# The instructions of a diffusion layer's kernel, scheduled on a timeline model of the machine instead of the default model

## The chip, the cores and the metric

The kernel runs on one core of a Trainium2 chip. The metric is the device time in microseconds (us) of one launch; the median of several runs is given.

## What is computed

One layer of a diffusion backbone for 512 latent tokens and 256 context tokens of 1024 features, in float32: a half-step SwiGLU feed-forward, a token mixer, another half-step feed-forward on the latent tokens, and a final norm. All norms are modulated from a conditioning vector. Cut to what matters:

```python
def swiglu(h, w_in, w_out):
    g, u = jnp.split(h @ w_in, 2, axis=-1)
    return (jax.nn.silu(g) * u) @ w_out

def step(S, xs):                                   # scan over the chunks of 64 tokens, 8 heads, two directions
    u_n, w_n, qd_n, kd_n, aqk_n, bl_n = xs
    v_new = u_n - jnp.einsum('bhcd,bhde->bhce', w_n, S)
    o = jnp.einsum('bhcd,bhde->bhce', qd_n, S) + jnp.einsum('bhij,bhje->bhie', aqk_n, v_new)
    S = S * bl_n[..., None, None] + jnp.einsum('bhcd,bhce->bhde', kd_n, v_new)
    return S, o

def merge_branches(p, pool_diff, o, pool_w, pool_scale, gdn_norm_w, w_gdn_proj, w_pool_proj, w_mix_out):
...
    o = rmsnorm(o.astype(dt), gdn_norm_w) * jax.nn.silu(gate)
    y_gdn = o.reshape(B, L, GDN_WIDTH) @ w_gdn_proj
...
    g_pool, g_gdn = jnp.split(jax.nn.sigmoid(p[..., POOL_END:]), N_BRANCH, axis=-1)
    return (g_pool * y_pool + g_gdn * y_gdn) @ w_mix_out
```

## The kernel before

Activations lie with the feature on the partition and the token along the row. Every large product is made in float32r: an operand is split into a high part (a cast, `hi`) and a low part (the rest, `lo`), and three matmuls make one product. For weights this is done by `halves` (L114): a transfer brings 128 columns into a staging tile (`stg`, `qst`), ScalarE casts them to `whi` (L119), VectorE, or for some GpSimd, subtracts and gives `wlo` (L120). There are four buffers of each. For activations `ahi` (L188) and `alo` (L189) do the same.

**The feed-forward half-steps** (`ffn`, L419) multiply 2 x 2 blocks by seven products (Winograd): `quad_weights` (L292) lets GpSimd form sums of weight blocks (`qs`, L308 to L313), `quad` (L337) issues the products (matmuls L345) and VectorE combines the results (L354 to L370). The activation between the two projections is VectorE and ScalarE work (L257, L260, L474, L188, L189). The first half-step has the modulation's matmuls (`ada_steps`, L141; L150, L157) strewn in; the second, on the latent tokens alone, runs from about 1400 us to the end, with matmuls of 256 columns.

**The mixer** treats eight heads. For a head, `head` (L589) projects and convolves q, k and v, `front` (L757) makes norms and transposes, `invert` (L802) inverts the chunks' small systems, `scan` (L938) runs six steps, one behind another, both directions side by side. In a step of the scan PE multiplies the state S by k (L952) and q (L963), VectorE forms R (L956), PE multiplies with the inverse (L973), VectorE weights it (`vw`, L976), PE multiplies with k again (L985), and VectorE adds the result to S (L994). Behind the last step the output is normed, transposed (L1014), gated (`y`, L1016) and stored to DRAM (L1017). The scan of head k, the front of head k+2 and the inversion of head k+1 are written interleaved; behind them, in the same turn of the loop, come the jobs: the projections of head k+3 (`head`), the gate of head k+1 (`gate`, L1021), and, of 16 branch gates (`branch_gates`, L1026), as many as a list says:

```python
    ORDER = "sfifsisiissiis"
    SHARE = (3, 2, 0, 0, 0, 0, 0, 0, 6, 5)
```

Each job is `job` (L123): 24 matmuls of 512 columns (L132) for each part of the tokens, out of weights that wait for nothing of the scan. Its matmuls write the banks `b`, those of the scan the banks `g`, those of front and invert the banks `a`. Behind the mixer, the outputs come back from DRAM and the projections follow (L1060 to L1116).

**What sets the order.** The kernel is recorded under a context of the tile framework. A scheduler takes the recorded instructions and gives each engine its own sequence: of those that are ready by its model of the machine an engine takes the one that was written first. The engines then run their sequences in order, and wait on semaphores. The order on the chip is therefore what the scheduler's model of durations makes of the program.

Of the kernel before, what the change touches and what calls it, by code (L numbers as in the profile page):

```python
# [13 lines left out]
PSUM = bass.MemoryType.PSUM  # L14
# [27 lines left out]
def layer_kernel(ctx, tc, a, out):  # L42
# [64 lines left out]
    def weights(src, k0, nk, c0, engs=(act, dve)):  # L107
        """128 columns of a matrix, in two float32r parts."""
# [5 lines left out]
    def halves(w, first=act, second=dve):  # L114
        """Up to four feature tiles of 128 columns, in two float32r parts."""
# [7 lines left out]
    def job(w, act_hi, act_lo, ks, parts, new=None):  # L123
        """One tile of 128 output features: w (K on the partition) times the activations."""
# [40 lines left out]
    def mod_scale(n, k, mod, rn):  # L165
        """(1 + scale) * norm weight for feature tile k."""
        dve.tensor_scalar(out=eff[:, n, k, :], in0=mods[:, mod * 8 + k, :], scalar1=1.0,
                          scalar2=vec[:, 0, rn + k:rn + k + 1], op0=ALU.add, op1=ALU.mult)
# [5 lines left out]
    def rstd_of(ssq, n, dim):  # L174
        """ssq: [128, n] sums of squares with the token on the partition."""
# [23 lines left out]
    def rstd_rows(tmp, acc, parts, ssq=None, tag="b", dtag=("diag", 1)):  # L199
        """Root mean square, inverted, of every token, the same on all partitions."""  # L200
# [29 lines left out]
    # [C11 C12; C21 C22] = [A11 A12; A21 A22] [B11 B12; B21 B22], rows: two tiles of 128 output features,  # L230
    # columns: two halves of the tokens, inner: two halves of the 8 feature tiles
    def products(n2, more):
        """The places of the right-hand operands: B11, B21, B22, T4, T1, T2, T3, and B12."""
# [9 lines left out]
    def blocks_of(t, k, n2, dst):  # L243
        """The blocks of B themselves, of feature tile k."""
# [3 lines left out]
    def blocks(dst):  # L248
        """The operands of the products of the blocks themselves."""
        return lambda j, part, k: dst[(0, 7)[j] if k < 4 else (1, 2)[j]][part][:, k % 4]  # L250

    def combine(tmp, b11, b12, b21, b22, n2, put, bufs=1, eng=dve):
        """The other right-hand operands from the blocks; overwrites b12, and without bufs b11 and b22."""
# [19 lines left out]
    def side_by_side(ws, outs, rhs, ks):  # L273
        """Products of several weights, one feature tile k of all of them after another."""
# [7 lines left out]
    def plain(src, c0, rhs, n2, k0=0, nk=KT, tags=None):  # L282
        """As quad, by eight multiplications, from the blocks themselves."""
# [8 lines left out]
    def quad_weights(tmp, deep, src, c0, rows=None):  # L292
        """256 columns of src on their way to the seven left-hand operands, in the order of their use."""
# [3 lines left out]
        for i in range(2):  # L297
            # the inner halves: the first and the last four feature tiles, or the even and the odd ones
# [21 lines left out]
    class Quads:  # L320
        """The quads of a list of (src, c0, rows), one after another."""
# [15 lines left out]
    def quad(quads, gen, w1, w6, rhs, n2):  # L337
        """Two tiles of output features of all tokens: C11 (in PSUM), C12, C21, C22."""
# [155 lines left out]
    def last_pair(ahi, alo):  # L494
        """The last two feature tiles' share of the output, first for the latents, and the mixer's input from it."""
# [93 lines left out]
    def head(h):  # L589
        """Project, convolve k, q and v of one head."""  # L590
# [8 lines left out]
    # columns of the small arrays: (direction, chunk, head); chunks 0-3 latent, 4-5 context  # L599
# [88 lines left out]
    with tc.tile_pool(name="pb", bufs=1, reuse_waits="tile") as pb:  # L688
        # the pooled projection with the token on the partition
# [48 lines left out]
    # one on the diagonal of every 32 x 32 block; one for the first 16 partitions of every 32  # L738
# [18 lines left out]
    def front(h):  # L757
        """Norms of k and q of one head, k and v with the token on the partition."""
# [472 lines left out]
```

## Time and profile before

| | us |
|---|---|
| runs of the kernel before | 1804.62, 1804.71, 1808.05 |
| median | 1804.71 |
| span of the profiled execution, first to last instruction | 1807.2 |
| mean granted TensorE clock in it | 0.961 |

The profile is of one execution; its span is given, not a device time of its own, and lies between the runs. Engines are PE (matmuls of TensorE), PEld (its weight loads), DVE (VectorE), ACT (ScalarE), POOL (GpSimd) and SP (which issues transfers). L132 is line 132 of the kernel. A clock of 1.00 is the full TensorE clock. A time in brackets behind an instruction is how long its engine stood idle before it, with what released it. Tiles are named by the program: `b<-hhi,whi` writes a bank b from hhi and whi. Matmuls are pipelined: their pace is read from start to start, not from the duration of one.

### The profile page before, as it was taken

To read this page: it belongs to the slowest core of one execution; us is meant where nothing else is said; L and a number is where in the kernel's file an instruction comes from. 1 tells how busy PE (TensorE), PEld (TensorE's weight loads), DVE (VectorE), ACT (ScalarE), POOL (GpSimd) and SP (SyncE) were. 2 spreads that over 40 slices of the span, in tenths; PEclk is the share of its full clock that TensorE was granted. 3 is DMA by queue.
4 is the path that set the end of the run, shared out by engine and by line. 5 is a ranking of instruction groups with operands and counts; after the bars stand their busy time and mean duration, and the time that the engine had idled before them with its cause. 6 is when DMAs were issued, how large, how long until landed. Compare 5 with 4: busy or idle time off the path is not lost.

```text
span 1807.2 us, 34927 instructions
## 1 busy us (share of the span) xinstructions
PE 1649.1 (91%) x13432; PEld 1486.5 (82%) x13432; DVE 1365.7 (76%) x2647; ACT 943.9 (52%) x2088; POOL 632.3 (35%) x669
## 2 busy tenths in 40 slices
PE   6899999999999999899999999999987888888886
PEld 4798998989999778777877888777877888888886
DVE  5778888897878874457776778645549899899886
ACT  5533343434344465757777776564426444444454
POOL 2244434444534020332233321100005556555642
PEclk9999999999999999999999999999998999899988
DMA  9455455351212353522221212247431222222221
GB/s 272 117 147 160 133 144 156 110 161 62 76 59 71 117 169 120 130 64 60 53 59 47 67 40 66 59 132 224 129 105 48 77 88 83 82 82 85 79 82 59
DMA packets 250971, 184.06 MB, mean 102 GB/s; under 512 B 7008, under 2 KB 238133, under 8 KB 250677
## 3 DMA queue, kind: packets, MB, share of 16 engines
q1 hardware_dynamic: 250368, 181.65, 34.4%
q8 instruction: 106, 1.74, 0.4%
q14 instruction: 60, 0.49, 0.1%
q10 hardware_dynamic: 437, 0.18, 0.0%
HBM read 170.22 MB, written 11.58 MB: 101 GB/s over the span
## 4 chain that ended last, share of the span: by engine, by line
PE 55%; DVE 25%; issue 6%; ACT 5%; DMA 5%; POOL 2%; SPq 0%; POOLq 0%; ACTq 0%; DVEq 0%
PE b L132 12%; PE b L345 11%; PE g L345 7%; PE a L345 6%; DVE wlo L120 4%; DVE cv L583 2%; DVE q L474 2%; DVE alo L189 2%; PE b L279 2%; DVE t L257 2%; DVE xT L437 1%; PE a L708 1%; PE a L132 1%; PE b L150 1%; PE g L132 1%
## 5 line engine op out<-in xcount | busy, mean ns | idle before, releaser
L119 ACT CAST whi<-qst 128x512 fp32r<-128x512 f32 (+2 forms) x288 | 159.1, 554 | 164.7 <-PE b L345 66.7
L120 DVE TENSOR_TENSOR wlo<-qst,whi 128x512 fp32r<-128x512 f32 (+2 forms) x288 | 215.5, 757 | 16.7 <-ACT whi L119 16.4
L119 ACT CAST whi<-qs 128x512 fp32r<-128x512 f32 (+2 forms) x216 | 117.7, 554 | 171.4 <-POOL qs L309 82.1
L132 PE MATMUL b<-hhi,whi 128*128 128x512 f32 (+1 forms) x528 | 188.4, 386 | 0.0
L132 PE MATMUL b<-hlo,whi 128*128 128x512 f32 (+1 forms) x528 | 188.3, 385 | 0.0
L132 PE MATMUL b<-hhi,wlo 128*128 128x512 f32 (+1 forms) x528 | 187.7, 386 | 0.0
L308 POOL TENSOR_TENSOR qs<-qst 128x512 f32<-128x512 f32 (+2 forms) x72 | 92.7, 1287 | 253.1 <-DMA qst<-in_ffn_w_in_dram 70.2
L313 POOL TENSOR_TENSOR qs<-qst,qs 128x512 f32<-128x512 f32 (+2 forms) x72 | 87.4, 1214 | 198.1 <-DVE wlo L120 181.1
L119 ACT CAST whi<-stg 128x512 fp32r<-128x512 f32 x154 | 94.3, 620 | 112.7 <-PE b L132 70.4
L120 DVE TENSOR_TENSOR wlo<-qs,whi 128x512 fp32r<-128x512 f32 (+2 forms) x144 | 104.9, 728 | 49.7 <-ACT whi L119 49.4
L345 PE MATMUL b<-ehi,wlo 128*128 128x384 f32 (+1 forms) x240 | 84.3, 351 | 45.7 <-DVE wlo L120 45.7
L179 POOL TENSOR_TENSOR rs<-rs,mhalf 128x4 f32<-128x4 f32 (+2 forms) x13 | 14.0, 1077 | 294.6 <-DVE rs L177 279.0
L188 ACT CAST ahi<-q 128x384 fp32r<-128x384 f32 (+1 forms) x118 | 55.3, 473 | 118.1 <-DVE q L474 60.8
L583 DVE SCALAR_TENSOR_TENSOR cv<-raw,vec,cv 128x772 f32<-128x772 f32 (+1 forms) x96 | 100.4, 1046 | 11.6 <-ACT cv L581 8.3
L345 PE MATMUL g<-hhi,whi 128*128 128x384 f32 (+1 forms) x320 | 105.5, 330 | 2.5 <-ACT whi L119 2.5
L345 PE MATMUL g<-hhi,wlo 128*128 128x384 f32 (+1 forms) x320 | 103.6, 324 | 3.6 <-DVE wlo L120 3.6
L132 PEld LDWEIGHTS b<-hlo,whi 128*128 128x128 f32 x528 | 94.6, 191 | 14.9
L132 PEld LDWEIGHTS b<-hhi,whi 128*128 128x128 f32 x528 | 94.5, 191 | 14.9
L132 PEld LDWEIGHTS b<-hhi,wlo 128*128 128x128 f32 x528 | 94.0, 191 | 15.0
L345 PE MATMUL g<-hlo,whi 128*128 128x384 f32 (+1 forms) x320 | 103.6, 324 | 0.0
L120 POOL TENSOR_TENSOR wlo<-stg,whi 128x512 fp32r<-128x512 f32 x46 | 65.4, 1429 | 90.6 <-ACT whi L119 70.5
L312 POOL TENSOR_TENSOR qst<-qst 128x512 f32<-128x512 f32 (+2 forms) x72 | 95.6, 1327 | 0.6
(480 smaller groups left out, 5459.6 us busy)
## 6 DMA issues: line engine op xcount, KB each, us to landing
qst<-in_ffn_w_in_dram SPq DMA_DIRECT2D x80, 512.0 KB, 3.5
stg<-in_w_ada_dram SPq DMA_DIRECT2D x56, 512.0 KB, 4.6
stg<-in_w_mix_in_dram SPq DMA_DIRECT2D x49, 512.0 KB, 3.9
qst<-in_ffn_w_out_dram SPq DMA_DIRECT2D x40, 256.0 KB, 2.7
adx<-in_w_ada_dram SPq DMA_DIRECT2D x16, 512.0 KB, 7.1
qst<-in_ffn_w_out_dram SPq DMA_DIRECT2D x16, 512.0 KB, 3.8
crow<-cumd SPq DMA_DIRECT2D x16, 384.0 KB, 8.8
stg<-in_ffn_w_in_dram SPq DMA_DIRECT2D x8, 512.0 KB
```

What stands on the lines that cost most here:

```text
L119: (first.copy if first is act else first.tensor_copy)(out=hi[:, :n], in_=w)
L120: second.tensor_tensor(out=lo[:, :n], in0=w, in1=hi[:, :n], op=ALU.subtract)
L132: pe.matmul(res[p][:, :m], lhsT=ww(i), rhs=hh(k)[:, o:o + m], start=(i == 0 and j == 0), stop=(i == n - 1 and j == 2))
L188: act.copy(out=hi, in_=src)
L189: dve.tensor_tensor(out=lo, in0=src, in1=hi, op=ALU.subtract)
L257: eng.tensor_tensor(out=t, in0=x, in1=y, op=ALU.subtract)
L279: pe.matmul(x, lhsT=ww(k), rhs=rhs(j, part, k), start=n + e == 0, stop=n + e == len(ks) + 1)
L308: pool.tensor_tensor(out=s1, in0=a21, in1=a22, op=ALU.add)
L312: pool.tensor_tensor(out=a21, in0=a11, in1=a21, op=ALU.subtract)
L313: pool.tensor_tensor(out=s2, in0=a12, in1=s2, op=ALU.subtract)
L345: pe.matmul(o, lhsT=ww[:, k], rhs=rhs(j, part, k), start=first and k + i == 0, stop=k + i == nh + 1, skip_group_check=not first)
L583: dve.scalar_tensor_tensor(out=cv[:, :n], in0=raw[:, t:t + n], scalar=tap[t], in1=cv[:, :n], op0=ALU.mult, op1=ALU.add)
```

## The change

One argument of the context in the last function is added; it makes the scheduler use a timeline model of the machine for its durations. No instruction of the program is changed. The rest of the diff takes out comments and descriptions of functions, with line numbers kept.

```diff
-    with tile.TileContext(nc) as tc:
+    with tile.TileContext(nc, schedule_with_timeline_sim=True) as tc:
         layer_kernel(tc, aps, o)
```

The new order differs on every engine. The names in the rows below are the program's tiles: `S`, `R`, `vw`, `vn` belong to the scan of a head, `kf` and `qf` are its k and q, `b` is the bank of a job, `hhi` and `hlo` are the normed activations that all jobs read.

PE, in the scan of head 7, one step of it, before:

```order
L952 MATMUL g_14203<-S_14199,kf_12571 128x128 x2
L963 MATMUL g_14209<-S_14199,qf_12648 128x128 x2
L132 MATMUL b_14343<-hhi_72,whi_14339 128x512
L132 MATMUL b_14343<-hlo_73,whi_14339 128x512
L973 MATMUL g_14214<-R_14206,L_13424 128x128 x2
L132 MATMUL b_14343<-hhi_72,wlo_14340 128x512
L132 MATMUL b_14381<-hhi_72,whi_14373 128x512
L132 MATMUL b_14381<-hlo_73,whi_14373 128x512
L132 MATMUL b_14381<-hhi_72,wlo_14374 128x512
L132 MATMUL b_14381<-hhi_72,whi_14373 128x512
L132 MATMUL b_14381<-hlo_73,whi_14373 128x512
L985 MATMUL g_14222<-vw_14217,kt_12820 128x128 x2
```

The same step on PE in the change:

```order
L952 MATMUL g_14203<-S_14199,kf_12571 128x128 x2
L963 MATMUL g_14209<-S_14199,qf_12648 128x128 x2
L973 MATMUL g_14214<-R_14206,L_13424 128x128 x2
L997 MATMUL g_14209<-vn_14219,aqk_13425 128x128
L985 MATMUL g_14222<-vw_14217,kt_12820 128x128 x2
L997 MATMUL g_14209<-vn_14219,aqk_13425 128x128
L952 MATMUL g_14232<-S_14225,kf_12571 128x128 x2
```

The job matmuls between the scan's are gone from here. They stand earlier: this is PE in the change where the last of the mixer's jobs ends, in the scan of head 4, ahead of its output (L1014):

```order
L132 MATMUL b_14495<-hhi_72,whi_14491 128x512
L132 MATMUL b_14495<-hlo_73,whi_14491 128x512
L132 MATMUL b_14495<-hhi_72,wlo_14492 128x512
L997 MATMUL g_12495<-vn_12503,aqk_11275 128x128 x2
L924 MATMUL a_12541<-U_12301,x2_12539 64x64 x6
L917 MATMUL a_12549<-TN_12300,L_12075 64x64 x6
L926 MATMUL a_12558<-x2_12556,U_12301 64x64 x6
```

Behind this row no L132 stands until the mixer's 600 remaining matmuls are through: the rest of scan 4 with its output, the scans of heads 5, 6 and 7, the inversions of 6 and 7 and the end of 5, the front of 7. In the order before, the jobs' matmuls (14 jobs of them) stand interleaved with these to the end. On DVE and ACT the jobs' work (L120, L583, L119, L1032) leaves this stretch likewise.

DVE in the second half-step, a piece of the difference, at the weight part `wlo_17275`, for which PE waits at 1513.83 in the trace before:

```order
+L120 TENSOR_TENSOR wlo_17275<-qst_17182,whi_17274 128x512
+L474 TENSOR_TENSOR q_16480<-q_16480,q_17092 128x256
 L260 TENSOR_TENSOR q_16564<-q_16517,q_16564 128x256
-L474 TENSOR_TENSOR q_16480<-q_16480,q_17092 128x256
 L257 TENSOR_TENSOR t2_17222<-q_16517,t1_17219 128x256
 L189 TENSOR_TENSOR alo_17208<-t1_17219,ahi_17207 128x256
+L120 TENSOR_TENSOR wlo_17306<-qst_17184,whi_17305 128x512
+L354 TENSOR_TENSOR q_17253<-q_17253,b_17238 128x256
 L189 TENSOR_TENSOR alo_17208<-q_16480,ahi_17207 128x256
 L189 TENSOR_TENSOR alo_17208<-q_16564,ahi_17207 128x256
-L189 TENSOR_TENSOR alo_17208<-t2_17222,ahi_17207 128x256
-L120 TENSOR_TENSOR wlo_17275<-qst_17182,whi_17274 128x512
```

The subtraction that gives `wlo_17275` stood behind seven instructions of the activation and now stands ahead of them; nine such places repeat this. In the first half-step the modulation's matmuls (L150, L157) are moved some 22 matmuls forward on PE and spread over more places. ACT loads its function table 15 times instead of 13.

## Rows read from the trace of the kernel before

**Rows 1.** The page, busy us, share of the span, instructions.
```profile
PE 1649.1 (91%) x13432; PEld 1486.5 (82%) x13432; DVE 1365.7 (76%) x2647; ACT 943.9 (52%) x2088; POOL 632.3 (35%) x669
```

**Rows 2.** Busy us (xcount) by stretch; then granted clock, DMA share, GB/s.
```profile
100.00:400.00 300.00, 292.79 (x2259) 279.87 (x2258) 251.04 (x513) 117.00 (x250) 133.45 (x119) 1.00 0.49 143
700.00:1232.00 532.00, 500.45 (x5516) 416.29 (x5515) 348.90 (x822) 367.40 (x941) 127.83 (x234) 0.99 0.29 78
1080.70:1220.30 139.60, 135.89 (x1455) 111.60 (x1454) 86.88 (x226) 87.30 (x225) 15.59 (x29) 1.00 0.29 86
1400.00:1500.00 100.00, 87.89 (x677) 86.14 (x678) 92.20 (x146) 47.21 (x98) 58.52 (x45) 0.93 0.28 85
...
1400.00:1807.20 407.20, 340.98 (x2594) 333.84 (x2594) 356.64 (x555) 191.48 (x383) 215.54 (x153) 0.90 0.26 80
```

**Rows 3.** Timeline of DVE, outputs of heads 4 and 7: start, us, engine, line.
```profile
1079.94 0.75 DVE L1016 SCALAR_TENSOR_TENSOR y<-g,vec,sgate 128x512 f32<-128x512 f32 x1 [2.25 <-PE g L1014]
...
1219.52 0.75 DVE L1016 SCALAR_TENSOR_TENSOR y<-g,vec,sgate 128x512 f32<-128x512 f32 x1 [3.74 <-PE g L1014]
```

**Rows 4.** Stretch between these outputs, instructions of L132 and then of L120 alone.
```profile
1080.70:1220.30 139.60, 88.53 (x302) 52.84 (x303) 1.00 0.29 86
...
1080.70:1220.30 139.60, 16.61 (x25) 0.00 (x0) 1.00 0.29 86
```

**Rows 5.** Timeline of PE behind head 7 (in brackets: idle before, releaser).
```profile
1220.48 0.40 PE L132 MATMUL b<-hlo,whi 128*128 128x512 f32 x1
...
1228.45 0.40 PE L132 MATMUL b<-hhi,wlo 128*128 128x512 f32 x1
1232.21 0.51 PE L132 MATMUL b<-yphi,whi 128*128 128x512 f32 x1 [3.36 <-ACT yphi L188]
```

**Rows 6.** Timeline of DVE, then of PE, in scan 7.
```profile
1194.97 0.42 DVE L994 TENSOR_TENSOR S<-S,g 128x256 f32<-128x256 f32 x1 [0.89 <-PE g L985]
...
1197.68 0.42 DVE L976 TENSOR_TENSOR vw<-g,w 128x256 f32<-128x256 f32 x1 [0.80 <-PE g L973]
...
1199.72 0.42 DVE L994 TENSOR_TENSOR S<-S,g 128x256 f32<-128x256 f32 x1 [0.70 <-PE g L985]
...
1195.54 0.68 PE L952 MATMUL g<-S,kf 128*128 128x128 f32 x4
...
1198.97 0.71 PE L985 MATMUL g<-vw,kt 128*128 128x128 f32 x4
```

**Rows 7.** A stretch of 20 us in which PE waits, columns as rows 2.
```profile
1340.00:1360.00 20.00, 12.77 (x49) 9.25 (x48) 9.90 (x19) 6.01 (x12) 2.65 (x3) 0.75 0.32 97
```

**Rows 8.** Waits of PE, 1400 to 1807 (total us, times, longest); its timeline.
```profile
PE b L345 <- DVE wlo L120: 40.1, 10, 4.8
...
1423.29 0.58 PE L345 MATMUL b<-ehi,wlo 128*128 128x256 f32 x1 [4.76 <-DVE wlo L120]
...
1719.58 0.58 PE L345 MATMUL b<-ehi,wlo 128*128 128x256 f32 x1 [4.26 <-DVE wlo L120]
```

**Rows 9.** Timeline of DVE, then of POOL, before 1513.83.
```profile
1502.09 0.42 DVE L474 TENSOR_TENSOR q<-q 128x256 f32<-128x256 f32 x1
...
1507.85 1.18 DVE L260 TENSOR_TENSOR q<-q 128x256 f32<-128x256 f32 x1
...
1510.35 1.48 DVE L257 TENSOR_TENSOR t<-q,t 128x256 f32<-128x256 f32 x1
...
1512.76 0.41 DVE L189 TENSOR_TENSOR alo<-t,ahi 128x256 fp32r<-128x256 f32 x1
1513.10 0.68 DVE L120 TENSOR_TENSOR wlo<-qst,whi 128x512 fp32r<-128x512 f32 x1
...
1504.46 1.41 POOL L313 TENSOR_TENSOR qs<-qst,qs 128x512 f32<-128x512 f32 x1 [4.22 <-DVE wlo L120]
...
1510.11 1.45 POOL L312 TENSOR_TENSOR qst<-qst 128x512 f32<-128x512 f32 x1
```

**Rows 10.** Waits of PE, 0 to 420 us.
```profile
PE b L150 <- DMA stg<-in_w_ada_dram: 1.5, 4, 0.6
```

## The prediction

> **What bounds the kernel now.** I start with the busy times of the whole span: TensorE's matmuls (PE) fill 91% of it, VectorE (DVE) 76%, ScalarE (ACT) 52% [rows 1]. That average covers two regimes, so the second view is the busy times by stretch. From 100 to 400 us (first feed-forward half-step) PE is busy 292.8 of 300 us. In the mixer, 700 to 1232, it is 500.5 of 532: 31.6 us idle. From 1400 to the end (second feed-forward half-step) it is only 341.0 of 407.2, and there DVE is the busier one with 356.6 [rows 2]. The third view, single instructions and their idle time, says why the mixer is dense although its scan is a chain that waits at every step: between the scan's small matmuls PE runs the large ones of `job` (L132), which need nothing of the scan. The output of head 4 (L1016) ends at 1080.7, that of head 7 at 1220.3 [rows 3]; between them there are 302 of these matmuls [rows 4], and 35 more behind head 7, the last at 1228.45 [rows 5].
>
> I take 1804.7, the median shown, as the base; the profiled span is 1807.2, 0.1% above. About 0.2% (3.6 us) is what a measurement of this kernel can tell from no change.
>
> **The change, part by part.** No matmul or vector instruction is added or removed, ACT gets two table loads more (no row prices them here; they are bounded by 0 and a few us, which the other ends swallow), so the whole effect is one of order.
>
> *1. The mixer's jobs run out early.* In the new order of PE the last L132 matmul of the mixer stands ahead of head 4's output transposes, and behind them come 600 matmuls of chains alone: scans 5, 6 and 7, inverts 6 and 7. So 302 + 36 matmuls move ahead of head 4's output. Their pace is (1228.45 − 1220.48)/34 = 0.234 us from start to start [rows 5], so they take 338 × 0.234 = 79 us. They can sink only into what PE has idle before: of the 31.6 us, 3.7 lie inside the tail itself (139.6 − 135.9) and 3.4 at the wait of 1232.21 [rows 2, 5]; that leaves 24.5, and I take half of it, since the rest stands where jobs were to be had already. Head 4's output thus ends 79 − 12 = **+67 us** later than 1080.7 (ends: +55 and +79).
>
> *2. The tail without cover.* The stretch from head 4's output to head 7's took 139.6 us [rows 2]; what would it take with the jobs gone? Below it can't fall under its own work: PE 135.9 − 302 × 0.234 = 65 us, DVE 86.9 less 16.6 for the jobs' weight splits (L120) = 70 [rows 2, 4]. Above stands its old length. Between these I read the step of scan 7 [rows 6]. From S at 1194.97 to S at 1199.72 is 4.75 us. In it the jobs delay the chain: vw ends at 1198.10, but its matmul L985 starts at 1198.97, 0.87 later, while L952, which waits for nothing else, starts at 1195.54, 0.15 after S ended at 1195.39. So 0.72 of a step of 4.75 is queueing behind jobs, and a step without them is 4.0, 0.84 of the old. I apply this to the whole tail: 0.84 × 139.6 = 117. [...] About half of a step is matmuls, so I add 5%: 123 us, and the tail gives back **−17 us** (ends: −64 at 75 us, +7 at 147).
>
> *3. Behind head 7* PE has 35 job matmuls left, then waits 3.36 for the reloaded y; the first projection starts at 1232.21 [rows 5]. Without jobs and with their weights long cast the next stage can begin sooner, unless the transfer of y sets it: **−4 us** (ends −8 and 0).
>
> *4. Second feed-forward half-step.* Nine times PE idles some 4.5 us at 128x256 matmuls `b<-ehi,wlo` because the weight part wlo (L120) isn't there; the first (4.76) and the last (4.26) of them are in [rows 8], and the view of waits counts 40.1 us in ten there, nearly all of it these nine. The wait's cause is in the row of DVE: wlo's subtraction itself takes 0.68 us but stands behind seven activation instructions, the first at 1507.85, the last at 1512.76 [rows 9]. The new DVE order puts the wlo ahead of them at all nine places. So the waits as they stand are ordered away, up to −40. But then DVE is late next: it would have to do its 356.6 us in 367, 97% busy, and no 100 us stretch of it that I read shows over 92.2% [rows 2]. At 92.2% its work takes 387, which is **−20 us**; I take that (ends: 0 and −40). DVE isn't free to be denser: an L257 instruction takes 1.48 us there while POOL runs, an L474 of the same shape 0.42 when POOL rests [rows 9].
> [...]
>
> *5. First feed-forward half-step.* The modulation matmuls (L150, L157), a compact block before, start about 22 matmuls sooner and are spread. PE waits for their transfer hardly at all now: 1.5 us in four waits, 0.6 the longest [rows 10]. If each of some 23 blocks in 100 to 400 waited 0.6, that would be +14; PE's idle time there is 7.2, which bounds a gain at −7. I take **+3**.
>
> **The sum**: 67 − 17 − 4 − 20 + 3 = +29, so 1804.7 + 29 = **1834 us**. It is slower because the jobs were not a load beside the scans but their filling: moved ahead, they lengthen a stretch that was full, and the chains that they leave are not much shorter for it.
>
> **The rivals.**
> *A, faster: the tail shrinks to its work.* If the chains of heads 5, 6 and 7 run side by side once no job stands between, the tail is set by DVE's 70 us, say 75 with joints, 48 less than forecast: 1834 − 48 = 1786. It decides at 123 − 29 = 94 us: a tail shorter than that makes the change faster. For it: DVE and ACT are lighter there by the jobs' casts. Against it: in the new order scan 6 begins behind scan 5's output, and a scan's six steps follow one another through S. Chance 0.09.
> *B, much slower: nothing is given back.* The tail keeps its 139.6 us with the 5% of a lower clock (147, 24 more), and the second half-step stays as long as it was, DVE being the bound there (20 more): 1834 + 24 + 20 = 1878. For it: the 0.75 of the clock at an idle PE [rows 7], and DVE at 88 to 92% [rows 2]. Against it: the jobs' queueing in front of L985 is real and ends. Chance 0.19.
> *C, no change: PE's work decides.* PE is at 91% [rows 1] and its work stays the same; idle time is merely dealt out otherwise, some in the mixer, less in the half-step behind, and the gain of step 4 meets the loss of steps 1 to 3 at 1805. It asks for a mixer loss of about 26, which is 20 less than mine (a tail of 103 us). Chance 0.06.
> [...]
>
> **How the numbers follow.** The forecast has 0.66, with a range of its own of 1812 to 1858 (the tail between 101 and 147, or step 4 between 0 and −40, one at a time); A 0.09, B 0.19, C 0.06. The range that leaves out the far half of A and of B, about 2 in 10 with the forecast's own misses, is 1800 to 1876. Faster by over 0.2%: A, 0.09. Within: C, 0.06. Slower: 0.85.
>
> **What would show it.** Right: no L132 between head 4's output (L1016) and head 7's; that output of head 4 at about 1148, head 7's at about 1270, the tail near 123 us with PE idle for half of it and a granted clock below 1; the nine waits on wlo shortened, DVE above 90% behind 1450. Wrong: a tail under 94 us (A), long waits `b<-ehi,wlo` still there under other names (B), head 4's output less than 40 us later, which would mean that PE had room before it, or new waits of L150 on its transfers in the first 400 us.

## The result and the profile after

The changed kernel takes 1945.3 us (median of 4 runs, 1940.6 to 1947.2); the kernel before took 1806.4 beside it. The ratio is 1.0756, 95% interval 1.073 to 1.078: slower, as forecast, but by 139 us where 29 were forecast, and outside the range of 1800 to 1876.

The page of the kernel after, its line of busy times (to be held against [rows 1]):

```profile
PE 1725.1 (89%) x13432; PEld 1532.4 (79%) x13432; DVE 1408.1 (72%) x2647; ACT 945.8 (49%) x2090; POOL 636.0 (33%) x669
```

The same 13432 matmul records are busy for 1725 us in place of 1649: no work was added, yet TensorE is busy 76 us longer. That goes with a lower granted clock (0.88 for 0.98 in the mixer), as the stretches show. Busy times by stretch of the kernel after, columns as in [rows 2]: the first feed-forward half-step, the mixer, 32 us inside the mixer, the stretch from head 4's output to head 7's, and two stretches of the second half-step:

```profile
100.00:400.00 300.00, 298.11 (x2196) 268.18 (x2195) 257.82 (x498) 114.61 (x243) 131.03 (x115) 1.00 0.47 139
600.00:1383.00 783.00, 673.83 (x6183) 565.19 (x6183) 433.63 (x983) 431.26 (x1041) 140.21 (x266) 0.88 0.25 72
953.00:985.00 32.00, 22.88 (x315) 19.58 (x315) 21.11 (x59) 16.44 (x43) 4.13 (x7) 0.73 0.15 42
1250.20:1382.60 132.40, 91.42 (x1104) 76.87 (x1102) 68.14 (x196) 63.11 (x170) 14.17 (x26) 0.71 0.09 31
1600.00:1700.00 100.00, 86.31 (x688) 83.85 (x688) 97.06 (x152) 47.83 (x102) 61.84 (x46) 0.98 0.29 93
1540.00:1944.90 404.90, 340.62 (x2651) 329.23 (x2649) 372.72 (x568) 193.38 (x394) 223.86 (x158) 0.95 0.26 81
```

and the mixer's stretch in the kernel before, with the same view:

```profile
585.00:1220.30 635.30, 598.75 (x6151) 500.69 (x6150) 427.90 (x979) 421.46 (x1034) 145.19 (x266) 0.98 0.30 85
```

The mixer is 783 us long in place of 635. PE's idle time in it rose from 36.5 to 109 us, and its busy time for the same matmuls from 599 to 674, at a granted clock of 0.88 in place of 0.98. So half of the 148 us shows as waits and half as longer busy time; what the lower clock costs the chain is read at experiment 8. DVE, in the second half-step, is now busy for 97% of a stretch of 100 us.

By stage, from the ends of the heads' outputs (L1016) and of the last L345 and L708 matmuls, before and after:

| | before | after | difference of the stage |
|---|---|---|---|
| first half-step ends (last L345) | 585.4 | 600.0 | +14.6 |
| last L708, before the heads | 697.7 | 739.1 | +26.8 |
| output of head 0 | 845.0 | 933.7 | +47.3 |
| output of head 3 | 1022.3 | 1156.8 | +45.8 |
| output of head 4 | 1080.7 | 1250.2 | +35.0 |
| output of head 7 | 1220.3 | 1382.6 | −7.2 |
| second half-step begins (first L345) | 1386.4 | 1540.6 | −8.1 |
| end | 1807.2 | 1944.9 | −16.5 |

Each column is one profile. The first half-step ended at 589.9 and 589.4 us in experiments 4 and 13, which leave it in the order of before, and at 597.6, 595.9 and 595.9 in 6, 8 and 15, which leave it in the order of the change: its difference is some 6 to 15 us. The stage between head 7's output and the second half-step took 162.4 us in 4 and 13, in the same order as the 166.1 above.

The rows for the outputs of heads 0, 4 and 7 in the kernel after, timeline of DVE (compare [rows 3]):

```profile
932.91 0.75 DVE L1016 SCALAR_TENSOR_TENSOR y<-g,vec,sgate 128x512 f32<-128x512 f32 x1 [0.40 <-PE g L1014]
...
1249.50 0.75 DVE L1016 SCALAR_TENSOR_TENSOR y<-g,vec,sgate 128x512 f32<-128x512 f32 x1
...
1381.84 0.75 DVE L1016 SCALAR_TENSOR_TENSOR y<-g,vec,sgate 128x512 f32<-128x512 f32 x1 [3.99 <-PE g L1014]
```

The loss arises before head 4's output. Two views of the kernel after say how: the matmuls of jobs alone (L132), over the period from head 0's output to head 1's and over 32 us in it (compare [rows 4]; columns PE, PEld, clock, DMA share, GB/s):

```profile
932.90:1006.60 73.70, 30.56 (x146) 23.62 (x147) 0.88 0.15 44
953.00:985.00 32.00, 0.64 (x3) 0.19 (x1) 0.73 0.15 42
```

The period has 146 job matmuls, nearly as many as before (158 in the period of 60.7 us), but none in its middle (the three counted there end by 953.7, the next starts at 988.0): for 32 us PE runs the chain alone, and it is busy there for 22.9 us only, at a granted clock of 0.73. The order of TensorE says the same. Between the outputs of heads 0 and 3 the jobs' matmuls stand in 79 runs of 5.6 on average before, with never more than 102 chain matmuls between two runs; in the change they stand in 28 runs of 15, with three stretches of some 170 chain matmuls, one to a head, without a job (a chain matmul leaves two records in the trace: the two L952 of a step are x4 in [rows 6]).

### The profile page after: what moved, and what is told of

The parts are those of the page before. It is cut to its first block, busy times and chain, and to the rows that moved or that the text cites. A ratio compares the mean times of both kernels' runs of the same rounds, so it can differ in the third digit from the quotient of the medians.

```text
span 1944.9 us, 34914 instructions
## 1 busy us (share of the span) xinstructions
PE 1725.1 (89%) x13432; PEld 1532.4 (79%) x13432; DVE 1408.1 (72%) x2647; ACT 945.8 (49%) x2090; POOL 636.0 (33%) x669
## 3 DMA queue, kind: packets, MB, share of 16 engines
q8 instruction: 106, 1.74, 0.4%
## 4 chain that ended last, share of the span: by engine, by line
PE 39%; DVE 14%; ACT 6%; issue 4%; DMA 2%; POOL 0%; SPq 0%; ACTq 0%; POOLq 0%; DVEq 0%
PE b L132 16%; PE b L345 4%; DVE wlo L120 3%; PE g L345 2%; PE a L345 2%; DVE q L474 1%; PE g L132 1%; PE g L973 1%; PE g L952 1%; PE a L708 1%; DVE alo L189 1%; PE a L132 1%; ACT din L848 1%; PE g L997 1%; PE g L985 1%
## 5 line engine op out<-in xcount | busy, mean ns | idle before, releaser
L120 DVE TENSOR_TENSOR wlo<-qst,whi 128x512 fp32r<-128x512 f32 (+2 forms) x288 | 250.0, 872 | 16.7 <-ACT whi L119 16.4
L119 ACT CAST whi<-qst 128x512 fp32r<-128x512 f32 (+2 forms) x288 | 157.9, 554 | 174.1 <-PE b L345 91.0
L132 PE MATMUL b<-hhi,whi 128*128 128x512 f32 (+1 forms) x528 | 189.6, 380 | 8.9 <-ACT cv L576 5.5
L132 PE MATMUL b<-hlo,whi 128*128 128x512 f32 (+1 forms) x528 | 187.3, 377 | 0.0
L119 ACT CAST whi<-qs 128x512 fp32r<-128x512 f32 (+2 forms) x216 | 118.0, 552 | 140.7 <-POOL qs L309 45.0
L132 PE MATMUL b<-hhi,wlo 128*128 128x512 f32 (+1 forms) x528 | 186.2, 376 | 0.0
L308 POOL TENSOR_TENSOR qs<-qst 128x512 f32<-128x512 f32 (+2 forms) x72 | 94.1, 1307 | 225.3 <-DMA qst<-in_ffn_w_in_dram 67.4
L119 ACT CAST whi<-stg 128x512 fp32r<-128x512 f32 x154 | 93.6, 619 | 93.0 <-PE b L132 58.7
L583 DVE SCALAR_TENSOR_TENSOR cv<-raw,vec,cv 128x772 f32<-128x772 f32 (+1 forms) x96 | 94.9, 988 | 43.2 <-ACT cv L581 19.4
L132 PEld LDWEIGHTS b<-hhi,whi 128*128 128x128 f32 x528 | 96.6, 191 | 29.2 <-ACT cv L576 7.3
L120 DVE TENSOR_TENSOR wlo<-stg,whi 128x512 fp32r<-128x512 f32 x108 | 75.1, 702 | 59.6 <-ACT whi L119 54.5
L120 DVE TENSOR_TENSOR wlo<-qs,whi 128x512 fp32r<-128x512 f32 (+2 forms) x144 | 105.3, 731 | 8.3 <-ACT whi L119 8.2
L132 PEld LDWEIGHTS b<-hhi,wlo 128*128 128x128 f32 x528 | 95.3, 191 | 17.0
L132 PEld LDWEIGHTS b<-hlo,whi 128*128 128x128 f32 x528 | 95.8, 191 | 16.4
L345 PE MATMUL g<-hhi,wlo 128*128 128x384 f32 (+1 forms) x320 | 101.2, 316 | 4.8 <-DVE wlo L120 4.8
L345 PE MATMUL g<-hhi,whi 128*128 128x384 f32 (+1 forms) x320 | 102.5, 320 | 1.9 <-ACT q L352 1.9
L345 PE MATMUL g<-hlo,whi 128*128 128x384 f32 (+1 forms) x320 | 100.5, 314 | 0.0
L312 POOL TENSOR_TENSOR qst<-qst 128x512 f32<-128x512 f32 (+2 forms) x72 | 100.2, 1392 | 0.6
L120 POOL TENSOR_TENSOR wlo<-qs,whi 128x512 fp32r<-128x512 f32 (+2 forms) x72 | 91.0, 1264 | 27.7 <-ACT whi L119 27.5
```

The lines of the kernel that those rows point to most:

```text
L119: (first.copy if first is act else first.tensor_copy)(out=hi[:, :n], in_=w)
L120: second.tensor_tensor(out=lo[:, :n], in0=w, in1=hi[:, :n], op=ALU.subtract)
L132: pe.matmul(res[p][:, :m], lhsT=ww(i), rhs=hh(k)[:, o:o + m], start=(i == 0 and j == 0), stop=(i == n - 1 and j == 2))
L308: pool.tensor_tensor(out=s1, in0=a21, in1=a22, op=ALU.add)
L312: pool.tensor_tensor(out=a21, in0=a11, in1=a21, op=ALU.subtract)
L345: pe.matmul(o, lhsT=ww[:, k], rhs=rhs(j, part, k), start=first and k + i == 0, stop=k + i == nh + 1, skip_group_check=not first)
```

## The experiments

Most kernels below take one of the two programs and fix the order of an engine in a stage to a table. The function is the same in all; the table is a list of the program's instruction numbers.

```python
    def follow(eng, names):
        """Issue the instructions of one engine in the order of this table (order alone, no wait)."""
        by = {i.name: i for i in nc.cur_bb.bb.instructions}
        seq = [by["I-%d" % n] for n in names if "I-%d" % n in by]
        for first, then in zip(seq, seq[1:]):
            tc.add_manual_dep(then, first.name,
                              mybir.DependencyInfo(mybir.DependencyClass.NoSync, mybir.DependencyReason.DATA),
                              reason="order")
```

What isn't in a table the scheduler of that kernel orders anew around it; this matters below.

**1 and 2. TensorE's order in the mixer, old in the new kernel and new in the old one.**

```diff
+    follow(None, table(ORDER_0))   # 1: TensorE, mixer, order of the kernel before; 2: of the changed kernel
```

> The changed kernel with TensorE's order in the mixer (3899 matmuls) fixed to that of the kernel before; all other engines and stages are scheduled by the timeline model. Theory A (TensorE's new order clusters the jobs' matmuls, so the chains run bare and at a lower clock): the mixer's 148 us come back, about 1797 us, between 1785 and 1815. Theory B (the new order of VectorE, ScalarE and the transfers slows the mixer): it stays above 1900.

> The kernel before with TensorE's order in the mixer fixed to that of the changed kernel, nothing else. Theory A: the mixer loses what it lost in the change, 148 us, about 1950 us, between 1925 and 1965. Theory B: below 1840.

Measured: 1875.3 and 1984.4 (ratios to before 1.036 and 1.097, intervals 1.032 to 1.041 and 1.092 to 1.102). Both miss the ranges of their theories; Theory A holds for the sign and not for the size. Putting TensorE's old order into the changed kernel gives back 70 us and not 148; putting the new one into the old kernel costs 177, more than the whole change. In experiment 1 the periods up to head 5's output are 62 to 71 us, near the old 56 to 61, but the stretch behind head 4 takes 154 us, against 139.6 before and 132.4 in the change: TensorE, in its old order, waits for results of VectorE and ScalarE, whose orders are new. The waits of PE in that kernel, 600 to 1304 us, its two largest:

```profile
PE g L952 <- DVE S L994: 14.6, 10, 2.7
PE g L997 <- ACT vn L980: 9.3, 8, 2.6
```

against 5.1 and 1.4 in the kernel before. An order of one engine carries a part of the effect. That a misfit with the others' orders comes on top is how these waits are read; no run isolates it.

**5 and 12. More engines' orders put back.** Both are kernel 1 with further tables.

```diff
     follow(None, table(ORDER_0))   # TensorE
+    follow(None, table(ORDER_1))   # VectorE (12); in 5 two tables more, for ScalarE and GpSimd
```

> The changed kernel with the order of TensorE, VectorE, ScalarE and GpSimd in the mixer fixed to that of the kernel before; transfers and the other stages stay as the timeline model orders them. With TensorE's order alone fixed, 69 us of the mixer's 148 stayed. Theory A (the orders of VectorE and ScalarE make the rest): about 1806 us, between 1795 and 1820. Theory B (the rest is in the transfers' order): above 1850.

> The changed kernel with the orders of TensorE and VectorE in the mixer fixed to those of the kernel before, ScalarE and GpSimd free. With TensorE alone 1875, with all four 1822. Theory A (VectorE is the partner whose order has to fit): below 1840. Theory B (it is ScalarE): above 1858.

Measured: 1822.6 with four engines (ratio 1.008, 1.005 to 1.011), 1853.9 with TensorE and VectorE (1.025, 1.021 to 1.028). With all four (just above the range of Theory A) the heads are what they were: periods of 58 to 61 us up to head 4, 139.4 from head 4 to head 7. The mixer as a whole takes 651 us, 16 more than before: 11 lie ahead of the heads and 5 up to head 0's output. So the engines' orders make some 132 of the mixer's 148 us, and at most the 16 are left for the transfers' order, which stayed new. Put back behind TensorE's, VectorE's order is worth 21 of the 53 us between kernels 1 and 5, ScalarE's and GpSimd's the other 31; neither theory of 12 is right alone.

**14. Jobs in lumps, in the old kernel.** TensorE's own old order, with the matmuls of each job put together.

```diff
+    follow(None, table(ORDER_0))   # TensorE, mixer: old order, each job's 24 or 48 matmuls at the place of the middle one
```

> The kernel before, with TensorE's order in the mixer fixed to its own, except that the matmuls of each of the mixer's jobs (24 or 48) stand together at the place of the middle one: 45 runs in place of 246. Nothing else is moved. Theory A (the fine interleaving is what hides the chains; a lump of 24 holds a chain step up by 5.6 us): 40 to 110 us slower, 1850 to 1920. Theory B (only the rough distribution of the jobs over the heads counts): within 15 us of 1807.

Measured: 1994.5 us, ratio 1.103 (1.101 to 1.105), 185 us slower: beyond the range of Theory A. A head's period is 77 to 83 us in place of 58 to 61, and the stretch from head 4 to head 7 is 188 in place of 140. Busy times of this kernel from head 1's output to head 2's, and from head 4's to head 7's:

```profile
976.60:1059.20 82.60, 67.94 (x686) 57.74 (x686) 43.78 (x102) 45.26 (x117) 17.69 (x29) 0.83 0.15 39
1216.50:1405.00 188.50, 158.48 (x1445) 130.44 (x1444) 86.04 (x222) 85.58 (x217) 15.41 (x29) 0.87 0.20 62
```

The number of matmuls is that of [rows 2] in the second stretch (x1445 against x1455), the jobs lie in the same places on the scale of a head, and PE is idle for 30 us and busy for 22 more. A run of 24 matmuls is 24 x 0.234 = 5.6 us [rows 5], longer than a whole step of the scan (4.75 us [rows 6]). What a chain step behind a run meets can be read in the kernel after, ahead of head 1's output: ScalarE has written vn (L981) at 989.50, but the L997 that takes it starts at 993.13, 3.63 us later, and in between PE is busy without a break with the matmuls ahead of it in the sequence, 17 L132 (988.01 to 992.25) and those of an inversion (from 992.18).

But more was moved than TensorE's matmuls. The other engines are ordered anew around the table: of the mixer's instructions only 76% on VectorE and 80% on ScalarE still stand in the succession of the kernel before (the longest that the two traces share; 95% and 98% in experiment 5). So the 185 us are the lumps together with the new orders around them, and no run parts the two.

**15. Jobs spread, in the new kernel.** The converse, for three heads.

```diff
+    follow(None, table(ORDER_0))   # TensorE, mixer: new order, 77 job matmuls of each period put in ones to threes into the bare chain
```

> The changed kernel with TensorE's order in the mixer fixed, but between the outputs of heads 0 and 3 the 77 job matmuls of each period that stood in runs ahead of a bare chain of 170 matmuls are spread over that chain, in ones to threes. Theory A (bunched jobs and bare chains run one after the other): each of the three periods falls from 74 us by 6 to 14, in all 1903 to 1927 us. Theory B (the periods are set by the orders of VectorE and ScalarE): periods of 70 us and more, above 1935.

Measured: 1931.7 us (ratio 1.068, 1.066 to 1.070), 14 us below the change. The three periods fell from 73.7, 76.3 and 73.1 to 67.4, 72.9 and 67.4, so by 6.3, 3.4 and 5.7: the right direction, the low edge or less of Theory A, and none near the 58 of before; the total lies between the two theories. The granted clock of the three periods went from 0.88, 0.80 and 0.88 to 1.00, 0.93 and 0.97. VectorE and ScalarE stay close to the change's orders here (93% and 95% by the count used for 14). So bunching on TensorE is a cause in the new order, for 15 of the 46 us lost between these outputs, and not the only one there.

**6 and 9. The last branch gates held for heads 5 to 7.** In 6 the first matmul of each of 11 gates is held behind a step of a scan, and the scheduler places the rest; in 9 the same 264 matmuls lie in 42 pieces where PE stood idle.

```diff
+    for step, gate_ in zip([...], [...]):          # 6: 11 scan matmuls, 11 first matmuls of a gate
+        tc.add_manual_dep(by["I-%d" % gate_], "I-%d" % step,
+                          mybir.DependencyInfo(mybir.DependencyClass.NoSync, mybir.DependencyReason.DATA), reason="order")
+    follow(None, table(ORDER_0))                   # 9 in its place: TensorE, mixer, the gates' matmuls in the gaps
```

> The changed kernel with the last 11 branch gates held on TensorE behind steps of scans 5, 6 and 7 (one edge of order each), so that they lie again between the chains. Theory A (the chains leave room that these 264 matmuls, 62 us, fill): head 4's output comes some 62 us sooner, the stretch from it to head 7's stays within 132 to 150 us, in all 1885 to 1905 us. Theory B (TensorE is no less busy for it, the chains slow down by what they cover): above 1930.

> The changed kernel with TensorE's order in the mixer fixed, and its 264 matmuls of the last 11 branch gates (62 us) taken out of it and put, in 42 pieces of 1 to 24, into the places where TensorE stood idle in the trace of heads 5 to 7 (39 us in all), in proportion to the idle time. Theory A (held in lumps of 24 they cost their full length, in pieces as long as the gaps they are nearly free): head 4's output some 46 us sooner, the stretch behind it 132 to 158 us, in all 1900 to 1925 us. Theory B (these matmuls cost their length wherever they stand, because other engines or the weights hold them): above 1935.

Measured: 1942.6 and 1930.0 us. In 6, head 4's output came 50 us sooner (the period 48.0 in place of 93.5), and the stretch behind it took it all back: 181.8 in place of 132.4. The gates, there in 25 runs of up to 24, cost as much as they had cost ahead of head 4. In the 42 pieces (9) the stretch behind head 4 grew by 14.8 us for the 62 of work, but head 4's output came only 29 us sooner; the total lies between the two theories, 15 us below the change. The finer cut cost less; it also lies in other places, so how much of this is the size of the pieces is not shown, nor that small pieces are nearly free.

**7. L997 behind L985 again.** In the new order one L997 stands ahead of L985 in the scan's steps.

```diff
+    follow(None, table(ORDER_0))   # TensorE, mixer: new order, in steps 2 to 4 of each scan L985 x2 ahead of L997 x2
```

> The changed kernel with TensorE's order in the mixer kept, but L997 (output matmuls of a scan step, waiting for ScalarE's vn) behind L985 (the state's) as it stood before; three steps of each of eight scans. Theory A (L997 in front holds the state's chain up by 0.5 to 0.8 us a step): 24 steps, 10 to 19 us faster, 1926 to 1936. Theory B (vn and vw come at the same time, or other waits end last): within 4 us of 1945.

Measured: 1953.6 us (1947.4 to 1956.0), no faster, rather 8 us slower: Theory A falls, and the 4 us of Theory B are passed too. The trace of this kernel says why, in scan 7: DVE's vw, ACT's two halves of vn, and PE's L985, now first in its queue:

```profile
1367.22 0.42 DVE L976 TENSOR_TENSOR vw<-g,w 128x256 f32<-128x256 f32 x1 [1.31 <-PE g L973]
...
1367.95 0.26 ACT L981 COPY vn<-g 128x128 f32<-128x128 f32 x1
...
1368.26 1.22 PE L985 MATMUL g<-vw,kt 128*128 128x128 f32 x4 [1.07 <-ACT vn L981]
```

vw ends at 1367.64, but L985 starts 0.62 us later, when ScalarE has read the second half of vn (1368.21). L985 takes no vn; it writes a bank `g`, of which there are two, and ScalarE must be through with its reads first. That last clause is the reading from the code; the release by L981 is the trace's.

**8. Filler matmuls for the clock.**

```diff
+        def fill(b, n):
+            for i in range(n if h >= 5 else 0):
+                pe.matmul(b[:, 256:512], lhsT=hhi[:, i % KT, 0:128], rhs=hhi[:, i % KT, 0:256], start=True, stop=True)
...
+                fill(b, 4)      # behind L952
+            fill(b, 6)          # behind L973
+                fill(b, 6)      # behind L985
```

> The changed kernel with 258 matmuls more of 128x256 in scans 5, 6 and 7, written to unused columns of the step's bank, behind L952, L973 and L985; they compute nothing that is used and keep TensorE busy while the chain waits, some 28 us of work. Theory A (the low granted clock, 0.71 in the stretch of heads 5 to 7, is a cause of its length): the stretch falls from 132 to 115 to 125 us though work is added, about 1930 us. Theory B (only the waits make its length): 132 to 150 us, 1945 to 1960.

Measured: 1953.9 us. Busy times of this kernel in the stretch from head 4's output to head 7's, and in the last scan alone:

```profile
1244.50:1391.40 146.90, 110.08 (x1356) 99.01 (x1354) 70.33 (x196) 63.57 (x170) 14.14 (x26) 0.89 0.08 28
1353.20:1391.40 38.20, 25.45 (x174) 21.70 (x173) 9.76 (x28) 11.84 (x36) 1.21 (x2) 0.95 0.26 90
```

The granted clock rose from 0.71 to 0.89, and in the last scan, where nothing but the chain is left, from 0.72 to 0.95. That scan took 38.2 us in place of 39.4, and the whole stretch grew from 132.4 to 146.9, as Theory B has it. So here the clock rose when work was put into TensorE's idle places. But the run doesn't tell what the clock costs, for the fillers held the chain up themselves: they write the bank that the next vector instruction reads. R in the last scan of this kernel, and in that of the change:

```profile
1368.63 0.35 DVE L961 SCALAR_TENSOR_TENSOR R<-g,necum,vt 128x128 f32<-128x128 f32 x1 [0.96 <-PE g L946]
...
1369.10 0.35 DVE L956 SCALAR_TENSOR_TENSOR R<-g,necum,vt 128x128 f32<-128x128 f32 x1 [0.47 <-PE g L952]
```

L946 is the filler; in the change R waits for the product of S and k alone. What the clock costs can be read in the kernel after by itself, which has steps of the scan with the same matmuls at a granted clock of 0.50 and of 1.00. Two steps of scan 6 and two of scan 7, none with a job between, then two of scan 7 with fillers (experiment 8):

```profile
1309.50:1322.20 12.70, 10.08 (x40) 8.94 (x40) 8.51 (x30) 3.69 (x12) 0.00 (x0) 0.50 0.00 1
1363.20:1372.50 9.30, 6.12 (x42) 4.91 (x40) 4.09 (x13) 3.06 (x10) 0.00 (x0) 1.00 0.00 0
...
1366.90:1380.10 13.20, 9.82 (x74) 8.68 (x72) 4.09 (x13) 3.06 (x10) 0.00 (x0) 1.00 0.00 0
```

The ends of these steps, where VectorE adds to S, in the kernel after:

```profile
1315.86 0.42 DVE L994 TENSOR_TENSOR S<-S,g 128x256 f32<-128x256 f32 x1 [0.72 <-PE g L985]
1322.22 0.42 DVE L994 TENSOR_TENSOR S<-S,g 128x256 f32<-128x256 f32 x1 [0.92 <-PE g L985]
...
1363.25 0.42 DVE L994 TENSOR_TENSOR S<-S,g 128x256 f32<-128x256 f32 x1 [1.50 <-PE g L985]
1367.87 0.42 DVE L994 TENSOR_TENSOR S<-S,g 128x256 f32<-128x256 f32 x1 [1.56 <-PE g L985]
```

From one L994 to the next a step takes 6.36 us at a granted clock of 0.50 and 4.62 at 1.00; with fillers it takes 6.59 at 1.00. L952, L973 and L985 take 1.06 to 1.23 us each at 0.50 and 0.61 to 0.71 at 1.00; L994 starts 0.11 us behind the end of L985 in both. So I read the 1.74 us by which the bare step at 0.50 is longer as the clock's, and experiment 8 gave with the clock what it took with the fillers. How much of the 75 us more of busy time in the mixer lengthened the chain was not isolated.

**3 and 11. The first half-step.** TensorE's new order in the old kernel, and the old one in the new.

```diff
+    follow(None, table(ORDER_0))   # 3: TensorE, first half-step, new order in the old kernel; 11: old order in the new kernel
```

> The kernel before with TensorE's order in the first half-step fixed to that of the changed kernel (modulation matmuls L150 in 72 groups in place of 36). Theory A (each further group costs a change of matmul kind, some 0.2 to 0.4 us): 8 to 15 us slower, 1814 to 1821. Theory B (VectorE's order and the transfers make the 14.6 us): within 4 us of 1806.

> The changed kernel with TensorE's order in the first half-step fixed to that of the kernel before (modulation matmuls in compact groups). Theory A (the split groups cost 14 us): 8 to 16 us faster, 1929 to 1937. Theory B (an order of one engine put among the others' new orders makes new waits, as in the converse run, which lost 38): slower than 1945.

Measured: 1846.7 and 1962.3 us, slower in both directions (37 over before, 17 over the change); the half-step took 519 us in both, against 500 before and 512.5 after, each from the first L345 to the last. Both theories of 3 miss. An order taken alone from another schedule costs more than either whole schedule, as Theory B of 11 says. How the change's own 14.6 us divide stays open. One part can be read: from the first L345 on L150 stands in 70 groups for 31, and a group of 8 in the timeline of PE after costs more than its share of a group of 32 before:

```profile
158.28 0.34 PE L345 MATMUL a<-ahi,wlo 128*128 128x384 f32 x1
158.54 0.43 PE L150 MATMUL b<-stg,sc 128*32 128x128 f32 x8
158.90 0.45 PE L345 MATMUL b<-ahi,whi 128*128 128x384 f32 x1
```

From L345 to L345 that is 0.62 us, of which 0.18 would pass without a group (158.10 to 158.28, the two L345 ahead): 0.44 for 8 matmuls. In the kernel before, 32 matmuls took 1.01 (163.03 to 164.04):

```profile
163.03 1.08 PE L150 MATMUL b<-stg,sc 128*32 128x128 f32 x32
164.04 0.44 PE L345 MATMUL g<-ahi,whi 128*128 128x384 f32 x1
```

so four groups of 8 cost some 0.7 us more than one of 32. From the start of each group to the next other matmul, all groups together take 35.8 us in place of 27.0.

**4, 10 and 13. The second half-step's gain, in the old kernel.**

```diff
+    follow(None, table(ORDER_0))   # 4: VectorE, second half-step
+    follow(None, table(ORDER_1))   # 13: with more tables also TensorE, ScalarE, GpSimd; 10: all five engines, from the output projections on
```

> The kernel before with VectorE's order in the second half-step fixed to that of the changed kernel. Theory A (the weight parts wlo moved ahead of the activation give the gain there): 12 to 20 us faster, 1786 to 1794. Theory B (the gain came from TensorE's or ScalarE's order, or from the stage ahead): within 4 us of 1806.

> The kernel before, with the orders of all five engines behind the mixer (output projections, second half-step, final norm) fixed to those of the changed kernel. VectorE's order alone gave nothing. Theory A (the orders of all engines together make the 24 us that the change gains there): 1776 to 1792 us, faster than both kernels. Theory B (the gain hangs on what was loaded and cast before the stage begins): above 1798.

> The kernel before, with the orders of VectorE, TensorE, ScalarE and GpSimd in the second half-step and final norm alone fixed to those of the changed kernel; the output projections keep the old order. With the projections' new order too, the half-step took 387 in place of 406 us, but the projections 180 in place of 166. Theory A (that loss lies at the seam ahead of the projections, the gain in the half-step stands by itself): 1785 to 1793 us. Theory B (a seam costs wherever it is cut): above 1800.

Measured: 4: 1807.6 us (ratio 0.999, 0.997 to 1.001); 10: 1808.5 (1.000, 0.999 to 1.001); 13: 1795.7 (0.9926, 0.991 to 0.994). VectorE's order alone gives nothing. With the projections' order too, the half-step, from its first L345 to its last, falls from 406 to 386.7 us (389.9 in the change), but the projections grow from 166 to 180, which I put down to the seam in front of them; no run shows it. Cut at the half-step itself the gain stays, 12 us in the half-step (394.3), and this version beats both kernels, by 0.7% the one before, just above the range of Theory A. Its projections took 162.4 us, but so did those of 4, in the same order. A seam can cost, but did not wherever it was cut.

## Why the prediction was wrong

*Step 1, the jobs that run out early (+67 forecast, +169.5 measured at head 4's output): this is the step that failed.* Its count and its price were right. Its sinking term was not, nor the premise under it that the heads ahead stay as dense as they were. L132 alone, in the kernel before, from 600 us to head 0's output, on to head 3's and on to head 4's:

```profile
600.00:845.00 245.00, 134.43 (x579) 99.29 (x579) 0.96 0.40 114
845.00:1022.30 177.30, 105.88 (x446) 72.07 (x446) 1.00 0.22 55
1022.30:1080.70 58.40, 33.21 (x138) 22.29 (x138) 1.00 0.20 49
```

and in the kernel after:

```profile
600.00:933.70 333.70, 175.94 (x824) 138.82 (x825) 0.94 0.35 99
933.70:1156.80 223.10, 94.15 (x424) 71.65 (x424) 0.85 0.16 44
1156.80:1250.20 93.40, 64.42 (x253) 46.22 (x253) 0.98 0.35 101
```

The sums are 1163 and 1501: 338 more, as counted, 79 us at 0.234. I took 12 us off, because the jobs would sink into idle time ("They can sink only into what PE has idle before"); that spoke of idle time as the old order left it. Measured, 169.5 less the first half-step's 14.6 less 79 leaves 76 us to be added. Up to head 0's output the stages lost 74.1 for 245 job matmuls more (57 us), so 17 beyond their price. From there to head 3's output there are 22 job matmuls fewer (5 us) and the stage is 45.8 longer: 51 us that moved work can't explain, and that go with a granted clock of 0.85 for 1.00 there. The period to head 4 lost 35.0 for 115 more (27 us). The largest part is thus where I looked for nothing: I took the heads before the fourth to stay dense, while the new order bunches the jobs in every head and runs a bare chain behind them. The order that I had would have told this, had I counted the runs between two heads' outputs and not only where the last job stands.

*Step 2, the tail without cover (−17 forecast, −7.2 measured: 132.4 us).* Within its range, but its working was wrong. I read the 0.87 us between vw and L985 [rows 6] as queueing behind jobs. The row of ScalarE in the kernel before, at that very place, shows what ended it:

```profile
1198.39 0.37 ACT L980 ACTIVATE vn<-g,bs 128x128 f32<-128x128 f32 x1
1198.65 0.27 ACT L981 COPY vn<-g 128x128 f32<-128x128 f32 x1
```

L981 ends at 1198.92 and L985 starts at 1198.97. The jobs were in front of L985 in the queue, but it could not have started sooner. In experiment 7, with no job there at all, the same wait is released by L981. At a granted clock of 1.00 a step of scan 7 in the change is 4.62 us (1363.25 to 1367.87 between two L994) against 4.75: the 4.0 that I worked out was not to be had, and taking the jobs out gave 0.13 us a step. The 5% that I added for a lower clock, in the 123 us and in rival B's 147, are a term that no run shows: the granted clock fell to 0.71 in the stretch, and at 0.50 a step with the same matmuls takes 6.36 us, 38% more (experiment 8). And I applied the step's share to the whole stretch, which holds more than steps. So that the total lies in its range is luck in part.

*Step 3, behind head 7 (−4 forecast, −8.1 measured)*: right in sign, just past the end of its bounds; against the 162.4 us of experiments 4 and 13 it is −4.4.

*Step 4, the second half-step (−20 forecast, −16.5 measured to the end)*: right in size. The cause was half right. Waits of PE in the kernel after, from 1540 us, the three largest (compare [rows 8]):

```profile
PE b L345 <- DVE wlo L120: 21.0, 11, 3.4
PE a L345 <- DVE q L358: 12.7, 13, 2.4
PE g L345 <- DVE wlo L120: 11.3, 9, 3.2
```

The waits on wlo for the bank b are halved (40.1 in [rows 8]), and a part came back as waits on other VectorE results, as forecast. DVE is 92% busy over the half-step now (372.7 of 404.9 us), as the forecast took it, though a stretch of 100 us shows 97%; and experiment 4 shows that VectorE's order isn't the gain by itself. The same instructions also took longer in one place than in another. The 11 L257 of one form in the half-step, before and after (busy us, mean ns, idle before):

```profile
L257 DVE TENSOR_TENSOR t<-q,t 128x256 f32<-128x256 f32 x11 | 16.1, 1460 | 0.0
...
L257 DVE TENSOR_TENSOR t<-q,t 128x256 f32<-128x256 f32 x11 | 8.6, 780 | 0.0
```

Before, all 21 L257 of the half-step lay beside a GpSimd instruction and took 1.22 us or more; after, the 7 that didn't took 0.41. The L120 lay beside GpSimd more often (72 of 182 rows of the timeline, 64 of 177 before), and their sum rose from 173 to 192 us. So the order changed what lies beside GpSimd.

*Step 5, the first half-step (+3 forecast, +14.6 measured, 6 to 15 by the other runs)*: about at its end of +14, and for another reason. New waits on the transfers of L150 were what I bounded; from the first L345 on they stayed at 1.5 us (ahead of it four new ones, on adx, came to 5.5). The smaller groups of L150 took some 9 us more; how the whole divides stays open.

*Between the steps*, the stage from the first half-step to the last L708 (+26.8 us, a part of the 74.1 above) was in no term of its own. Experiment 5, with four engines' orders back, still has 11 of it.

Of the rivals, A asked for a tail under 94 us and got 132; B named a tail that gives nothing back, which is near, but priced it at 1878; C fell, and its sum was wrong: a mixer loss of 26 with −20 and +3 gives 1814, and no change asks for a loss of 17, a tail of 94 us, which is where A begins.

The cause as far as the runs carry it: the loss in the mixer is made by the engines' orders (experiment 5 gives back 132 of 148 us), TensorE's among them for about half (1). Bunching the jobs is shown as a cause in the changed kernel: spreading them over three heads gave 14 us in all and raised the clock there (15). How much of the rest is bunching, lower clock or a misfit between the engines' orders was not isolated; experiment 14 moves the other engines too.

## What to carry to other kernels

When a scheduler moves work between dependent chains, count the lengths of the runs on the engine that the chains share with it, between two fixed points of the chain, and not only where the last piece stands: a run that is longer than a step of the chain (5.6 us against 4.75 here) can delay it where a short one covers it. When a matmul starts late behind others in its queue, look which instruction on another engine ended just before it, since a full queue can hide what the instruction would have waited for anyway, here ScalarE's L981, which ended 0.05 us before L985 started. To price a lower clock, compare steps with the same matmuls at different granted clocks in one trace, here 6.36 us at 0.50 and 4.62 at 1.00; work added to raise the clock may hold up the chain that it is to speed up. Take an order over for a whole stage and all engines at once; one engine's share of it may cost more than either whole order.

## What the runs showed that was not expected

- Filler matmuls lifted the granted clock from 0.71 to 0.89 over 147 us and lengthened the chain's step by about as much as the clock shortened it: 6.59 us with fillers at a granted clock of 1.00, against 6.36 at 0.50 and 4.62 at 1.00 without them (experiment 8 and the kernel after).
- VectorE was 97% busy over 100 us beside a GpSimd at 62%, after 92% with 59% before, and in the half-step an L257 took 0.41 us without a GpSimd instruction beside it and 1.1 to 1.5 with one.
- One engine's order, taken from the other schedule, was slower in both directions (experiments 3 and 11: +37 and +17 us), though the two schedules differ by 14.6 us in that stage.
